# The adaLN gate of a hybrid attention layer: from matmul rows on TensorE to column sums on VectorE and GpSimd

## The chip, the core and the metric

The kernel runs on one NeuronCore of a Trainium2 chip. The metric is the time of one execution on the device in microseconds (us). The profile is one further execution, recorded instruction by instruction. In it PE is TensorE (matmuls), DVE is VectorE, ACT is ScalarE, POOL is GpSimd and SP is SyncE, which here only issues transfers (DMA). Each engine works through its own instructions strictly in order; an instruction that waits holds up all that stand behind it on that engine.

## What is computed

One layer of a diffusion backbone: 128 context tokens and 1024 latent tokens, width 1024, each with its own conditioning vector. The part that matters here is the modulation: a vector is passed through SiLU, multiplied by a 1024 x 3072 matrix, and split into shift, scale and gate. Shift and scale act on the input; the gate is used only at the very end.

```python
def modulation(cond, w_mod, b_mod):
    m = (jax.nn.silu(cond) @ w_mod + b_mod)[..., None, :]
    shift, scale, gate = jnp.split(m, 3, axis=-1)
    return shift, scale, gate

    shift, scale, gate = modulation(c, w_mod[l], b_mod[l])
    h = rmsnorm(xs, norm_gain[l]) * (1.0 + scale) + shift
    q_a, k_a, v_a, g_a, q_b, k_b, v_b, g_b = project(h, w_in[l], ...)
    ...
    xs = xs + gate * merge_out(o_a, g_a, o_b, g_b, w_out[l])
```

The same is done for the context tokens with `c_ctx`. So the gate is two vectors (for `c` and `c_ctx`) of 1024 numbers, each a sum over 1024 products. All is fp32.

## The kernel before

Nine token tiles of 128 rows (tile 0 is the context). Projections are made with fp32r operands split in a high and a low part: three matmuls for each of eight slices of the width, 24 matmuls of 128x128 by 128x512 for one *block* (a token tile by 512 columns). The stages are: modulation, norm and the first gates; the queries of mixer A (first sweep, `m = 0`, nine blocks) and of mixer B (second sweep, `m = 1`, nine blocks); keys and values; the second gates; then attention with the output projection. The gate of the adaLN is worked out inside the two query sweeps, where the pool `qt` is open, is written to a row in DRAM (`gate_row`), and is read back (L1057) for the output.

The order of work is written by hand. `block` (L267 ff.) calls `tick` twice, before its first and before its second half, so **a tick is half a block**; the first sweep has ticks 1 to 18 and the second 19 to 36. `later(n, f)` puts `f` into the list of the tick that is n ahead; a tick runs its list in the order in which entries were made. `in_order` at the end fixes each engine's order as the program wrote it.

A query, after its block, goes through `query` (L586 ff.):

- in the next tick (odd) ACT squares the block's result (`sqq`, L594), DVE sums the squares (`ssq`, L596) and scales them (`ms`, L171), and POOL takes the power -1/2 (`rs`, L173);
- two ticks on (odd) DVE multiplies the result by it (`qn`, L601, from PSUM), and by the rope tables (`ra`, L531, and `rb`, L537, both from SBUF);
- the tick after (even) DVE adds the two (`qf`, L612, from SBUF);
- three ticks after that (odd) PE transposes it, four 128x128 transposes into one bank (`ptq`, L622), ACT copies the bank out as the high part (`qo0`, L625) and DVE one tick later takes the low part (`qo1`, L630, from PSUM); both go to DRAM by transfers that ACT issues (L635). The transposes use two banks D and E in alternation (`bank_tr`), so a transpose waits until DVE has read the bank two before it.

In an odd tick DVE's order is therefore `qn`, `ra`, `rb` of one query, then `ssq`, `ms` of the next; in an even tick `qf` and `qo1`. In the last block of a sweep the weights of the next one are split as well (`Weights.split`, L229): ACT casts the high part, DVE subtracts for the low one (L235), eight times; PE needs each in the block that follows.

The gate before the change: SP loads the gate's weights as four tiles of 1 MB (`load_wg`, two early in the first sweep, two in the second) and the biases. Ahead of the fourth and the eighth block of the second sweep, `gate_rows` makes eight matmuls with the SiLU vectors as weights padded to 32 columns, four side by side, into a bank; a tick later ACT copies it out; three ticks later `gate_sum` adds the four groups with one more matmul (`pgs`, into a bank of D and E), DVE adds the bias (`bg`), and SP writes half the row.

## Time and profile before

| | us |
|---|---|
| Runs: median (lowest to highest of 3) | 723.14 (722.96 to 723.36) |
| Profiled execution, first to last instruction | 721.3 |
| The rest of the median, outside of that span | 1.8 |
| PE busy | 698.3 |
| DVE / ACT / POOL busy | 457.6 / 411.7 / 335.3 |
| Gate matmuls on PE: `pgate` 32 passes, `pgs` 4 passes | 2 stretches of 1.92, 2 of 1.02 |

The page reads the profiled execution: busy time, its share of the span, and the number of instructions for each engine. A row of the timeline is the start, the duration, the engine, the source line, the operation, output and input tiles, shapes and, in brackets, how long the engine had been idle before it and what it had waited for. "x4" merges four instructions that follow each other. A row of a group gives the count, the summed busy time and the mean in ns, and then the idle time ahead of it. The granted TensorE clock was 0.993 of full speed on average.

### The profile page before, as it was taken

The page shows a single profiled execution, that of the slowest core. Times are in us where ns is not written, and L with a number is a line of the kernel's source. Part 1 is how long each engine was busy: PE and PEld are TensorE (multiplying, and loading weights), DVE is VectorE, ACT ScalarE, POOL GpSimd, SP SyncE. Part 2 cuts the span into 40 slices and gives each one's busy share as a digit, 9 for nine tenths or more (in the row PEclk, how much of TensorE's full clock was granted, in tenths as well). Part 3 has the DMA queues.
Part 4 walks back from the last instruction along what each step waited for, and adds up shares of the span by engine and source line. Part 5 has one row for each costly group of instructions (what it writes and reads, how often), then busy time and mean ns, then how long its engine had stood idle before and what let it go on. Part 6 is the DMA issues. An engine that isn't in the chain of part 4 may idle for free. (4 is left out here: it accounts for less than half of the span.)

```text
span 721.3 us, 10622 instructions
## 1 busy us (share of the span) xinstructions
PE 698.3 (97%) x3524; PEld 559.7 (78%) x3524; DVE 457.6 (63%) x1007; ACT 411.7 (57%) x829; POOL 335.3 (46%) x355
## 2 busy tenths in 40 slices
PE   5999999999999999999999999999999999999997
PEld 2678988877777788977788888888888888887865
DVE  3466147875675872745866677577666775775653
ACT  5355411411232451158778877877787778877770
POOL 3456013332322340236666555655575557555751
PEclk9999999999999999999999999999999999999999
DMA  8961373348435115440321222121212221212323
GB/s 344 346 219 59 121 278 86 79 94 276 121 85 142 45 60 171 139 143 23 103 67 45 73 67 88 44 81 52 87 54 59 66 87 45 81 53 87 103 65 119
DMA packets 53159, 78.56 MB, mean 109 GB/s; under 512 B 6569, under 2 KB 25449, under 8 KB 52081
## 3 DMA queue, kind: packets, MB, share of 16 engines
q1 hardware_dynamic: 44928, 65.96, 28.1%
q10 hardware_dynamic: 8176, 11.94, 6.3%
q8 instruction: 28, 0.46, 0.3%
q14 instruction: 27, 0.21, 0.1%
HBM read 58.69 MB, written 19.18 MB: 108 GB/s over the span
## 5 line engine op out<-in xcount | busy, mean ns | idle before, releaser
L1108 POOL TENSOR_TENSOR pl<-pe,ph 128x512 fp32r<-128x512 f32 x130 | 167.6, 1292 | 144.7 <-DVE nm L919 67.5
L859 DVE TENSOR_REDUCE mx<-pmx 128x1 f32<-128x384 f32 x192 | 101.4, 552 | 59.5 <-PE pmx L858 58.1
L1100 ACT ACTIVATE pe<-st 128x512 f32<-128x512 f32 x146 | 86.8, 594 | 28.0 <-PE st L1098 27.1
L1104 ACT CAST ph<-pe 128x512 fp32r<-128x512 f32 x146 | 90.6, 621 | 4.8
L1118 PE MATMUL pv<-ph,v_hi 128*128 128x512 f32 x208 | 83.2, 400 | 2.2 <-DVE spare L1142 2.2
L1121 PE MATMUL pv<-pl,v_hi 128*128 128x512 f32 x208 | 82.6, 397 | 0.0
L173 POOL TENSOR_TENSOR rs_q<-ms_q,mhalf 128x8 f32<-128x8 f32 x18 | 34.8, 1931 | 82.1 <-DVE ms_q L171 82.1
L1189 PE MATMUL po<-wo,ogh 128*128 128x512 f32 x216 | 72.5, 394 | 0.2 <-DVE yt L1196 0.2
L919 DVE CUSTOM_DVE_ANT_0 sn<-sn,mask,nsink 128x512 f32<-128x512 f32 (+1 forms) x64 | 46.3, 724 | 38.3 <-PE sn L916 36.5
L858 PE MATMUL pmx<-kha,qt 128*128 128x384 f32 x192 | 61.0, 363 | 0.4 <-ACT pen L905 0.2
L1097 PE MATMUL st<-qt,kha 128*128 128x512 f32 x144 | 58.3, 405 | 1.5 <-ACT pe L1100 0.8
L1098 PE MATMUL st<-qb,kla 68*128 68x512 f32 x144 | 57.6, 400 | 1.1 <-DVE qb L878 1.1
L1120 PE MATMUL pv<-ph,v_lo 128*64 128x512 f32 x146 | 57.9, 396 | 0.0
L1121 PEld LDWEIGHTS pv<-pl,v_hi 128*128 128x128 f32 x208 | 39.4, 189 | 16.7 <-issue 0.2
L905 ACT ACTIVATE pen<-sn,nm 128x512 f32<-128x512 f32 (+2 forms) x72 | 45.0, 626 | 6.5 <-DVE nm L919 3.1
L1093 ACT CAST ph<-st 128x512 fp32r<-128x512 f32 x62 | 36.4, 587 | 19.9 <-PE st L1092 18.7
L1118 PEld LDWEIGHTS pv<-ph,v_hi 128*128 128x128 f32 x208 | 39.4, 189 | 10.5 <-ACT ogh L1154 2.4
L1189 PEld LDWEIGHTS po<-wo,ogh 128*128 128x128 f32 x216 | 40.0, 188 | 6.8 <-DVE yt L1196 0.6
L1094 DVE TENSOR_TENSOR pl<-st,ph 128x512 fp32r<-128x512 f32 x62 | 42.5, 686 | 2.3 <-ACT ph L1093 1.5
L1189 PE MATMUL po<-wo,ogl 128*128 128x512 f32 x108 | 42.6, 394 | 0.0
L594 ACT ACTIVATE sqq<-pq 128x512 f32<-128x512 f32 x18 | 10.8, 599 | 53.3 <-DMA qd<-qo0q 14.4
L858 PEld LDWEIGHTS pmx<-kha,qt 128*128 128x128 f32 x192 | 35.5, 190 | 6.2 <-DVE mx L859 1.4
(216 smaller groups left out, 1700.2 us busy)
## 6 DMA issues: line engine op xcount, KB each, us to landing
qt<-qd SPq DMA_DIRECT2D x36, 256.0 KB, 3.1
wm<-in_w_mod_ss_dram SPq DMA_DIRECT2D x8, 1024.0 KB, 5.1
qd<-qo0q ACTq DMA_DIRECT2D x36, 128.0 KB, 2.4
qd<-qo1q ACTq DMA_DIRECT2D x36, 128.0 KB, 2.4
sgl<-gd SPq DMA_DIRECT2D x36, 128.0 KB, 2.1
out_dram<-yt SPq DMA_DIRECT2D x17, 256.0 KB, 2.1
xn<-in_x_sample_dram SPq DMA_DIRECT2D x8, 512.0 KB, 7.0
wg<-in_w_mod_g_dram SPq DMA_DIRECT2D x4, 1024.0 KB, 7.9
```

Source lines behind the costliest of these rows:

```text
L858: nc.tensor.matmul(pm[:, 0:384], lhs, kha[:, g, 3 * b : 3 * b + 3, :], start=True, stop=True)
L859: nc.vector.tensor_reduce(mx[:, h, b : b + 1], pm[:, 0:384], axis=AX.X, op=ALU.max)
L919: nc.vector.tensor_tensor_reduce(s, s, mask[:, m0 : m0 + n], -1.0, nsink[:, 4 * g + h : 4 * g + h + 1], op0=ALU.add, op1=ALU.min, accum_ou ...
L1097: nc.tensor.matmul(s, kh, qtile[i], start=True, stop=False)
L1098: nc.tensor.matmul(s, kl, qbtile[i], start=False, stop=True)
L1100: nc.scalar.activation(pe, s, AF.Exp)
L1104: nc.scalar.copy(ph, pe)
L1108: nc.gpsimd.tensor_tensor(pl, pe, ph, op=ALU.subtract)
L1118: nc.tensor.matmul(pv, two, ph, start=(b == 0), stop=False)
L1120: nc.tensor.matmul(pv[0:64, :], vl, ph, start=False, stop=False)
L1121: nc.tensor.matmul(pv, two, pl, start=False, stop=last)
L1189: nc.tensor.matmul(po[n], a, wo_parts[KT * n + k][lo], start=(k == KS[0] and p == 0), stop=(k == KS[-1] and p == 2))
```

## The change

The gate leaves TensorE, apart from one transpose. The host hands the gate's part of the weights over transposed, with the two conditioning vectors appended as rows. Tile `wg{j}` then has 128 gate columns as partitions and the 1024 inputs along the row, and a gate column is a sum along the row. `silb` holds both conditioning vectors on all partitions (two loads of 512 KB, SiLU on ACT in ticks 3 and 4). For j = 0 to 7, in tick 6 + 3j (6, 9, 12, ... 27), `gate_columns(j)`:

- asks for the tile of the next column (`load_wg(j + 1)`, for j of 1 to 6; two buffers);
- on DVE multiplies and sums for `c` in one instruction (its result and a read of the accumulator are two rows);
- on POOL multiplies for `c_ctx` into `prod`, which ACT copies two ticks later, summing on the way.

In tick 30 DVE adds the biases; in tick 31 PE transposes the 16 columns (`ptg`, a bank of D and E), ACT copies them out and SP writes `gate_row`.

```diff
-GATE_AT = (3, 7)
+GATE_AT = (6, 3)
...
-        sil32 = qt.tile([P, KT, 32], F32, name="sil32g", bufs=1)
...
-        def gate_sum(n, grow):
-            pgs = bank_tr(f"pgs{n}")
-            nc.tensor.matmul(pgs[0:2], sel, grow, start=True, stop=True)
-            nc.vector.tensor_tensor(bg[n], pgs[0:2], bg[n], op=ALU.add)
-            nc.sync.dma_start(gate_row[:, 512 * n : 512 * n + 512], bg[n])
-        def gate_rows(n):
-            pg = bank_mm(f"pgate{n}")
-            for k in range(KT):
...
+        silb = qt.tile([P, 2, D], F32, name="silb", bufs=1)
+        gcol = qt.tile([P, 2, KT], F32, name="gcol", bufs=1)
+        gbias = qt.tile([P, KT], F32, name="gbias", bufs=1)
+        for c in range(2):
+            nc.sync.dma_start(silb[:, c], w_mod_g[D + c : D + c + 1, :].to_broadcast([P, D]))
+        nc.sync.dma_start(gbias, cols[:, 40:48])
+        wg = {}
+
+        def load_wg(j):
+            wg[j] = qt.tile([P, D], F32, tag="wg", name=f"wg{j}")
+            nc.sync.dma_start(wg[j], w_mod_g[P * j : P * j + P, :])
+
+        def gate_silu(c):
+            nc.scalar.activation(silb[:, c], silb[:, c], AF.Silu)
+
+        def gate_columns(j):
+            if 0 < j < KT - 1:
+                load_wg(j + 1)
+            junk = qt.tile([P, D], BF16, tag="junk", name=f"junk{j}", bufs=1)
+            nc.vector.tensor_tensor_reduce(junk, wg[j], silb[:, 0], 1.0, 0.0, op0=ALU.mult, op1=ALU.add,
+                                           accum_out=gcol[:, 0, j : j + 1])
+            prod = qt.tile([P, D], F32, tag="prod", name=f"prod{j}", bufs=1)
+            nc.gpsimd.tensor_tensor(prod, wg[j], silb[:, 1], op=ALU.mult)
+            later(2, lambda: nc.scalar.activation(prod, prod, AF.Copy, accum_out=gcol[:, 1, j : j + 1]))
+
+        def gate_turned():
+            pt = bank_tr("ptg")
+            nc.tensor.transpose(pt[0:16, 0:P], gcol.rearrange("p c j -> p (c j)"), ident_r.bitcast(F32))
+            grow = qt.tile([16, P], F32, name="grow", bufs=1)
+            nc.scalar.copy(grow, pt[0:16, 0:P])
+            nc.sync.dma_start(gate_row.rearrange("c (j n) -> (c j) n", n=P), grow)
+
+        for j in range(2):
+            load_wg(j)
+            later(3 + j, lambda j=j: gate_silu(j))
+        for j in range(KT):
+            later(GATE_AT[0] + GATE_AT[1] * j, lambda j=j: gate_columns(j))
+        end = GATE_AT[0] + GATE_AT[1] * (KT - 1) + 3
+        later(end, lambda: nc.vector.tensor_tensor(gcol, gcol, gbias.unsqueeze(1).to_broadcast([P, 2, KT]), op=ALU.add))
+        later(end + 1, gate_turned)
...
-                if m == 1 and t in (ts[GATE_AT[0]], ts[GATE_AT[1]]):
-                    gate_rows(len(wg) // 2 - 1)
...
-    return {"cols": cols, "w_mod_ss": ss, "w_mod_g": w_mod[0][:, 2 * D :]}
+    return {"cols": cols, "w_mod_ss": ss, "w_mod_g": np.concatenate([w_mod[0][:, 2 * D :].T, c.reshape(1, D), c_ctx.reshape(1, D)])}
```

Since the entries for the columns are made before any query's, a column stands first in its tick on DVE and POOL. Three places show what that does to the order. In the names, the number behind `q0_` or `q1_` is the token tile, and the last number is a running one that differs between the programs.

DVE, in the last block of the first sweep (ticks 17 and 18), before:

```order
L596 TENSOR_REDUCE ssq0_8_1514<-sqq0_8_1512 128x8
L171 TENSOR_SCALAR ms_q0_8_1516<-ssq0_8_1514 128x8
L235 TENSOR_TENSOR wloqb_0_1530<-rawqb_0_1416,whiqb_0_1529 128x512
L235 TENSOR_TENSOR wloqb_1_1537<-rawqb_1_1418,whiqb_1_1536 128x512
L612 TENSOR_TENSOR qfq0_7_1540<-ra_q0_7_1505,rb_q0_7_1507 128x2x4x64
L630 TENSOR_TENSOR qo1q0_5_1499<-ptq0_5_1493,qo0q0_5_1498 128x512
L235 TENSOR_TENSOR wloqb_2_1547<-rawqb_2_1420,whiqb_2_1546 128x512
L235 TENSOR_TENSOR wloqb_3_1554<-rawqb_3_1422,whiqb_3_1553 128x512
```

and with the change:

```order
L608 TENSOR_REDUCE ssq0_8_1539<-sqq0_8_1537 128x8
L171 TENSOR_SCALAR ms_q0_8_1541<-ssq0_8_1539 128x8
L235 TENSOR_TENSOR wloqb_0_1555<-rawqb_0_1434,whiqb_0_1554 128x512
L235 TENSOR_TENSOR wloqb_1_1562<-rawqb_1_1436,whiqb_1_1561 128x512
L576 ISA junk4_1567,gcol_1092<-wg4_1454,silb_1091 128x1024
L576 ISA gcol_1092 128x1
L624 TENSOR_TENSOR qfq0_7_1571<-ra_q0_7_1529,rb_q0_7_1531 128x2x4x64
L642 TENSOR_TENSOR qo1q0_5_1523<-ptq0_5_1517,qo0q0_5_1522 128x512
L235 TENSOR_TENSOR wloqb_2_1578<-rawqb_2_1438,whiqb_2_1577 128x512
L235 TENSOR_TENSOR wloqb_3_1585<-rawqb_3_1440,whiqb_3_1584 128x512
```

The fifth column (`junk4`, and the read of its sum) has come between the second and the third of the weights' low parts.

POOL, over the same stretch of the first sweep and into the second, before (powers alone):

```order
L173 TENSOR_TENSOR rs_q0_5_1325<-ms_q0_5_1323,mhalf_106 128x8
L173 TENSOR_TENSOR rs_q0_6_1380<-ms_q0_6_1378,mhalf_106 128x8
L173 TENSOR_TENSOR rs_q0_7_1461<-ms_q0_7_1459,mhalf_106 128x8
L173 TENSOR_TENSOR rs_q0_8_1518<-ms_q0_8_1516,mhalf_106 128x8
L173 TENSOR_TENSOR rs_q0_0_1605<-ms_q0_0_1603,mhalf_106 128x8
```

and with the change:

```order
L173 TENSOR_TENSOR rs_q0_5_1342<-ms_q0_5_1340,mhalf_106 128x8
L579 TENSOR_TENSOR prod2_1360<-wg2_1257,silb_1091 128x1024
L173 TENSOR_TENSOR rs_q0_6_1403<-ms_q0_6_1401,mhalf_106 128x8
L579 TENSOR_TENSOR prod3_1458<-wg3_1356,silb_1091 128x1024
L173 TENSOR_TENSOR rs_q0_7_1485<-ms_q0_7_1483,mhalf_106 128x8
L173 TENSOR_TENSOR rs_q0_8_1543<-ms_q0_8_1541,mhalf_106 128x8
L579 TENSOR_TENSOR prod4_1569<-wg4_1454,silb_1091 128x1024
L173 TENSOR_TENSOR rs_q0_0_1636<-ms_q0_0_1634,mhalf_106 128x8
```

Two of three powers are followed by a product of 1024 elements a partition.

DVE in ticks 29 and 30 with the change, ahead of PE's transpose of the columns in tick 31 (before, `gcol` is not there and the rest stands in the same order):

```order
L608 TENSOR_REDUCE ssq1_5_1922<-sqq1_5_1920 128x8
L171 TENSOR_SCALAR ms_q1_5_1924<-ssq1_5_1922 128x8
L595 TENSOR_TENSOR gcol_1092<-gcol_1092,gbias_1093 128x16
L624 TENSOR_TENSOR qfq1_4_1941<-ra_q1_4_1912,rb_q1_4_1914 128x2x4x64
L642 TENSOR_TENSOR qo1q1_2_1906<-ptq1_2_1900,qo0q1_2_1905 128x512
```

The bias add now stands ahead of the `qf` and `qo1` of tick 30, and PE's `ptg` of tick 31 needs it; `ptg` takes one of the two banks, so the transposes `ptq1_3` behind it take the bank that this `qo1q1_2` reads.

On SP the change puts `silb` (two loads), the biases and two tiles of `wg` ahead of the first sweep's rope tables; the loads of `wg2` and `wg3`, which wait for their buffers, ahead of the second sweep's weights; and the write of `gate_row` in tick 31 ahead of the 16 loads of the key and value weights.

More of the change, by code (lines that the diff above doesn't have):

```diff
@@ L553, in hybrid_step @@
             w.pools = [(qt, KT)] * KT
-        sil32 = qt.tile([P, KT, 32], F32, name="sil32g", bufs=1)
-        nc.gpsimd.memset(sil32, 0.0)
-        nc.vector.tensor_copy(sil32[:, :, 0:2], silc.rearrange("p (c k) -> p k c", c=2))
-        sel = qt.tile([P, 2], F32, name="selg", bufs=1)
-        group_sum(sel, ident_r.bitcast(F32))
-        wg, bg = [], []
-        def gate_sum(n, grow):
-            pgs = bank_tr(f"pgs{n}")
-            nc.tensor.matmul(pgs[0:2], sel, grow, start=True, stop=True)
-            nc.vector.tensor_tensor(bg[n], pgs[0:2], bg[n], op=ALU.add)
-            nc.sync.dma_start(gate_row[:, 512 * n : 512 * n + 512], bg[n])
@@ L569, in gate_rows @@
-        def gate_rows(n):
-            pg = bank_mm(f"pgate{n}")
-            for k in range(KT):
-                a = 32 * (k % 4)
-                nc.tensor.matmul(pg[a : a + 32], sil32[:, k, :], wg[2 * n + k // 4][:, k % 4, :],
-                                 start=(k < 4), stop=(k >= 4), tile_position=(0, a))
-            grow = qt.tile([P, 512], F32, tag="grow", name=f"grow{n}", bufs=1)
-            later(1, lambda: nc.scalar.copy(grow, pg))
-            later(3, lambda: gate_sum(n, grow))
@@ L579, in load_wg @@
-        def load_wg(i):
-            n, b = divmod(i, 2)
-            wg.append(qt.tile([P, 4, 512], F32, tag="wg", name=f"wg{i}"))
-            nc.sync.dma_start(wg[i], w_mod_g[512 * b : 512 * b + 512, 512 * n : 512 * n + 512].rearrange(
-                "(k p) n -> p k n", p=P))
+        silb = qt.tile([P, 2, D], F32, name="silb", bufs=1)
[3 more added lines that the diff above has]
+            nc.sync.dma_start(silb[:, c], w_mod_g[D + c : D + c + 1, :].to_broadcast([P, D]))
@@ L646, in hybrid_step @@
                 pq = bank_mm(f"pq{m}_{t}")
-                if m == 1 and t in (ts[GATE_AT[0]], ts[GATE_AT[1]]):
-                    gate_rows(len(wg) // 2 - 1)
-                if (m, t) in ((0, ts[-2]), (1, ts[GATE_AT[0]])):
-                    n = len(wg) // 2
-                    load_wg(2 * n)
-                    load_wg(2 * n + 1)
-                    if n == 0:
-                        bgt = qt.tile([34, 512], F32, name="bg", bufs=1)
-                    bg.append(bgt[32 * n : 32 * n + 2])
-                    nc.sync.dma_start(bg[n], b_mod[:, 2 * D + 512 * n : 2 * D + 512 * n + 512].to_broadcast([2, 512]))
                 if t == ts[-2]:
```

## The prediction

> **What bounds the kernel now.** I read the page first, then the timeline of TensorE (PE) over the query stage (about 89 to 202 us), then VectorE (DVE), GpSimd (POOL) and ScalarE (ACT) over the same stretch.

> ```profile
> PE 698.3 (97%) x3524; PEld 559.7 (78%) x3524; DVE 457.6 (63%) x1007; ACT 411.7 (57%) x829; POOL 335.3 (46%) x355
> ```

> PE sets the end. A projection block is 24 matmuls; the turn of an earlier query (four transposes, `ptq`, L622) opens it, so the starts of the turns are PE's clock:

> ```profile
> 111.09 0.60 PE L622 MATMUL ptq<-ident_r,qfq 128*128 128x128 f32 x4
> 117.03 0.60 PE L622 MATMUL ptq<-ident_r,qfq 128*128 128x128 f32 x4
> ...
> 153.03 0.60 PE L622 MATMUL ptq<-ident_r,qfq 128*128 128x128 f32 x4
> 159.05 1.92 PE L573 MATMUL pgate<-wg,sil32g 128*32 128x512 f32 x16
> 160.90 0.66 PE L622 MATMUL ptq<-ident_r,qfq 128*128 128x128 f32 x4
> 166.88 0.60 PE L622 MATMUL ptq<-ident_r,qfq 128*128 128x128 f32 x4
> 167.64 1.02 PE L565 MATMUL pgs<-grow,selg 128*2 128x512 f32 x2 [0.15 <-DVE qo1q L630]
> ...
> 174.19 0.60 PE L622 MATMUL ptq<-ident_r,qfq 128*128 128x128 f32 x4
> 180.12 0.60 PE L622 MATMUL ptq<-ident_r,qfq 128*128 128x128 f32 x4
> 187.99 0.66 PE L622 MATMUL ptq<-ident_r,qfq 128*128 128x128 f32 x4
> 193.98 0.60 PE L622 MATMUL ptq<-ident_r,qfq 128*128 128x128 f32 x4
> 201.76 0.63 PE L622 MATMUL ptq<-ident_r,qfq 128*128 128x128 f32 x4 [0.47 <-DVE qo1q L630]
> ```

> A plain block lasts 117.03 - 111.09 = 5.94 us. I call the turns 1 to 18 in this order: turn 1 at 111.09, turn 6 opens the second sweep, turn 7 is six blocks after turn 1.

> DVE does five rows of 0.6 to 0.7 us a query, and one wait:

> ```profile
> 113.88 0.69 DVE L601 TENSOR_TENSOR qnq<-pq,rs_q 128x512 f32<-128x512 f32 x1 [1.53 <-POOL rs_q L173]
> 114.60 0.69 DVE L531 TENSOR_TENSOR ra_q<-qnq,tcos 128x512 f32<-128x512 f32 x1
> ...
> 115.88 0.68 DVE L596 TENSOR_REDUCE ssq<-sqq 128x8 f32<-128x512 f32 x1
> 116.60 0.17 DVE L171 TENSOR_SCALAR ms_q<-ssq 128x8 f32<-128x8 f32 x1
> 116.68 0.69 DVE L612 TENSOR_TENSOR qfq<-ra_q,rb_q 128x512 f32<-128x512 f32 x1
> 117.28 0.68 DVE L630 TENSOR_TENSOR qo1q<-ptq,qo0q 128x512 fp32r<-128x512 f32 x1
> 118.89 0.69 DVE L601 TENSOR_TENSOR qnq<-pq,rs_q 128x512 f32<-128x512 f32 x1 [0.93 <-POOL rs_q L173]
> ...
> 122.39 1.94 POOL L173 TENSOR_TENSOR rs_q<-ms_q,mhalf 128x8 f32<-128x8 f32 x1 [3.54 <-DVE ms_q L171]
> ```

> Its loop is 118.89 - 113.88 = 5.01 us: from `ms` to `qn` 2.29 (POOL's power takes 1.94 of it), then `qn`, `ra`, `rb`, `ssq`, 2.72. So DVE has 0.93 us a block in hand, and no more.

> **What goes.** Four blocks held gate matmuls. Their length over 5.94: 153.03 to 160.90 gives 1.93; 166.88 to 174.19, 1.37; 180.12 to 187.99, 1.93; 193.98 to 201.76, 1.84 (0.47 of it a wait for a bank whose turn `pgs` had shifted). Together **-7.07 us** of PE's own time. Nothing else of it was on PE's path.

> **What comes, priced.**

> ```profile
> L919 DVE CUSTOM_DVE_ANT_0 sn<-sn,mask,nsink 128x512 f32<-128x512 f32 x48 | 36.4, 757 | 27.0 <-PE sn L916 26.8 <-ACT pen L905 0.2
> L919 DVE CUSTOM_DVE_ANT_0 sn<-sn,mask,nsink 128x384 f32<-128x384 f32 x16 | 10.0, 624 | 11.3 <-PE sn L916 9.7 <-ACT ph L1104 1.4
> ...
> L1144 POOL TENSOR_TENSOR spare<-spare,sgl x36: 730/738/746, 341.2 to 703.2; 128x256 f32<-128x256 f32 x36
> ...
> L382 ACT ACTIVATE sq<-xn x9: 1044/1056/1057, 8.0 to 43.6; 128x1024 bf16<-128x1024 f32 x9
> L382 ACT ACTIVATION_READ_ACCUMULATOR sq<-xn x9: 186/187/198, 9.0 to 44.6; 128x1 f32 x9
> ```

> The multiply-and-sum of a column block on DVE is the same instruction as L919 on 1024 elements: 757 + 4 x (757 - 624) = 1.29 us. A plain two-input operation gives a floor: twice L531's 0.69, 1.38, less one fixed part. I take **1.25** from start to next start. The ceiling is twice the streamed part, 2.3, if this operand mix runs at half the rate; no row here has it. ACT's summing copy is 1.06 + 0.19 = 1.25 us and each SiLU about the 1.06; ACT is 57% busy and its copies fall into its waits for PE, or delay the squares by 1.25, which DVE, later still, doesn't feel. POOL's product has 1024 elements: 512 take 1.29 (rows below), 256 take 0.74, so 1.29 + 2 x 0.55 = **2.4 us**, at most 2 x 1.29 = 2.58.

> POOL itself has room: 1.94 + 2.4 fit in a block. But what it does to DVE is in these rows of the attention stage:

> ```profile
> 356.67 1.66 DVE L1015 TENSOR_TENSOR wo_big<-wraw,wo_big 128x512 fp32r<-128x512 f32 x1
> 358.26 0.75 DVE L919 CUSTOM_DVE_ANT_0 sn<-sn,mask,nsink 128x512 f32<-128x512 f32 x1
> 358.93 1.15 DVE L1014 CAST wo_big<-wraw 128x512 fp32r<-128x512 f32 x1
> ...
> 356.45 1.33 POOL L1108 TENSOR_TENSOR pl<-pe,ph 128x512 fp32r<-128x512 f32 x1 [1.34 <-ACT ph L1104]
> 358.50 1.29 POOL L1108 TENSOR_TENSOR pl<-pe,ph 128x512 fp32r<-128x512 f32 x1 [0.72 <-ACT ph L1104]
> ```

> A DVE subtraction of two SBUF tiles, 0.69 elsewhere, takes 1.66 when POOL began first, and a 0.42 us cast takes 1.15: both end a little after POOL's operation does. L919, with one input in PSUM, keeps its 0.75. So while a product runs, DVE's operations on two SBUF tiles stand still: `ra`, `rb`, `qf`, the tables, the weights' low parts, and the new columns. `qn` and `qo1` read PSUM and go on.

> **DVE's loop with a column.** The power ends 2.26 after `ms`. A tick is half a block; columns come every third tick. Even tick: column, `qf`, `qo1` fill the wait; the product runs from 2.26 to 4.66, so `ra` starts at 4.7 in place of 3.0: **6.7 us**. Odd tick: `qf`, `qo1`, column end at 2.55; the product then runs to 4.95: **7.0 us**. Three blocks carry two columns: 6.7 + 7.0 + 5.0 = 18.7 against PE's 17.8. DVE falls behind by 0.9 in three blocks, and by more at the places that follow.

> *First sweep.* The two rope tables now stand behind 2 MB of gate input on SP.

> ```profile
> 99.99 0.68 DVE L546 TENSOR_TENSOR tcos<-tcos,gain 128x512 f32<-128x512 f32 x1
> ...
> 106.56 0.17 DVE L171 TENSOR_SCALAR ms_q<-ssq 128x8 f32<-128x8 f32 x1
> ...
> wg<-in_w_mod_g_dram SPq DMA_DIRECT2D x4, 1024.0 KB, 7.9
> ```

> 1 MB lands in 7.9 us among others; part passes while DVE waits anyway. Bounds 0 and 6 us; I take 2.3. The second `ms` is then at 108.9, and the next ones at 115.6, 122.6, 127.6, 134.3, 141.3 (loops even, odd, plain, even, odd). Turn 3 needs the `qo1` that ends 1.3 behind the ms of 122.6: 123.9, against 122.97 on PE (two blocks after 111.09); turn 4 needs column, `qf`, `qo1` behind 127.6: 130.15, against 129.8; turn 6 needs `qf`, the second tables (1.2 us) and `qo1` behind 141.3: 143.8, against 140.8 today (five blocks after 111.09). Late by **3.0**.

> *The weights' low parts.* This is the largest term.

> ```profile
> 139.96 1.29 DVE L235 TENSOR_TENSOR wloqb<-rawqb,whiqb 128x512 fp32r<-128x512 f32 x2
> ...
> 142.38 3.69 DVE L235 TENSOR_TENSOR wloqb<-rawqb,whiqb 128x512 fp32r<-128x512 f32 x6
> ...
> 143.11 0.50 PE L249 MATMUL pq<-wloqb,h 128*128 128x512 f32 x1
> ...
> 137.27 1.21 ACTq L635 DMA_DIRECT2D qd<-qo1q  x2
> ...
> 139.02 4.25 ACT L233 CAST whiqb<-rawqb 128x512 fp32r<-128x512 f32 x8
> ```

> Already PE waits for the third low part (143.11: 0.3 late). Column 4 now stands between the second and third. `qn` starts at 143.8, so the eighth `ms` is at 146.5: two low parts to 147.8, the column to 149.05; POOL, whose power ended at 148.8, takes the inputs until 151.45; `qf` and `qo1` to 152.65; the third low part at 153.3. PE, which now takes it at 143.11, is 10.2 late: **7.2 more**. (Without any blocking this place costs 2.5: 1.25 for the column, 1.25 for ACT's copy between `qo0` and the issues of 137.27.)

> *The turn of the columns.* `gate_turned` sits ahead of turn 12 and takes a bank in the alternation, so turn 12 needs the `qo1` of the tick just before. The six low parts end at 156.4; counted on, the ms are at 159.1, 163.1 (the context query has no rotation), 169.4 (its power waits for a product, then ACT's squares), 176.1, 183.1, 188.1. Bias add, `qf` and `qo1` end at 189.5; PE, 10.2 late at turn 7, is there at 157.3 + 5 x 5.94 = 187.0: **2.5**, the transpose within it.

> *After it* the second boundary looks like the first does now: **0.4** (147.09 - 140.76 - 5.94).

> *SP.* The KV weights wait behind the gate's row:

> ```profile
> 171.47 9.84 SPq L221 DMA_DIRECT2D rawkv<-in_w_in_dram  x16
> ```

> Begun 0.5 us after turn 12, all 16 are out 10.3 after it, and land some us later; ACT's first cast comes two blocks and 4.2 us after it (139.02 is 4.2 behind its turn), 16.1. Hidden, with about 4 us to spare.

> **Sum.** -7.07 + 3.0 + 7.2 + 2.5 + 0.4 = **+6.0**. The profiled span is 721.3, the median of the runs 723.14, 1.8 more. 721.3 + 6.0 + 1.8 = **729.1 us**. Bounds: start 0 gives about 727, start 6 gives 733; a product of 2.58 adds 0.2 a column, 1.5; the order in which DVE and POOL get the inputs moves 0.6 at the boundary. Own range 725 to 735.

> **Rivals.**

> *The column runs at half rate* (14%). For it: no row has two fp32 SBUF tiles with a running sum; L919 has PSUM and bf16. Against: L531 streams two SBUF tiles at full rate. At 2.3 us the loops are 8.6 and 8.0, turn 6 comes at 149.5, the third low part at 160.1 (17.0 late), turn 12 waits 6.2: -7.1 + 17.0 + 6.2 + 0.4 = +16.5, **739.6 us**. [...]

> *The product doesn't hold DVE* (13%), the other side: if the product costs DVE's loop less than (17.8 - 15.0) / 2 = 1.4 us a column, DVE keeps PE's pace. Left are 0.3 at the start, 2.5 at the boundary, 1.75 at turn 12, 0.4: -7.07 + 4.95 = -2.1, **721.0 us**. For it: POOL's power never slowed `qf` (0.69 throughout). Against: power reads 8 elements, the product 1024, like L1108.

> *The loads come late* (5%): SP's later loads wait for columns to be read, and KV's stand behind the gate row. From 4 us of lateness on each us is PE's: 8 late gives **733**.

> **Chances.** Forecast 68% (725 to 735). Faster by over 0.2% (what a measurement can tell here, 1.4 us): most of the second rival and the low tail, 14%. Within 0.2%: 6%. Slower: 80%. Range 722 to 738, leaving out about 20%.

> **What would show it.** `ra` rows of 2 us and more behind a product; the third `wloqb` about 10 us later than now; turns 3, 4, 6 and 12 waiting for DVE, 7 the most; PE idle for some 13 us more, half of it before that `wloqb`. It is wrong if `ra` stays 0.69 and starts 0.7 after `qn`, or if the columns last 2.3.

## The result, and the profile after

The changed kernel takes **736.69 us** (median of four runs, 735.19 to 737.48), the kernel before 723.14 (722.96 to 723.36). The ratio is 1.0179, with a 95% interval of 1.0158 to 1.0199: slower, by 13.5 us. The profiled execution of the changed kernel took 735.19 us, with a span of 733.4, which is 12.1 more than the 721.3 of the profile before; it was the fastest of the four.

The page of the changed kernel, first the busy time of each engine:

```profile
PE 695.2 (95%) x3489; PEld 559.3 (76%) x3489; DVE 475.5 (65%) x1018; ACT 421.2 (57%) x846; POOL 356.7 (49%) x362
```

PE is busy for 3.1 us less and the span is 12.1 us longer, so PE is idle for some 15 us more. The timeline of PE over the query stage shows where (columns: start, length, operation; in brackets the idle time ahead of it and what ended it). The turns are counted as in the prediction.

```profile
111.88 0.63 PE L634 MATMUL ptq<-ident_r,qfq 128*128 128x128 f32 x4 [1.64 <-issue]
...
124.87 0.66 PE L634 MATMUL ptq<-ident_r,qfq 128*128 128x128 f32 x4 [0.95 <-DVE qo1q L642]
131.68 0.66 PE L634 MATMUL ptq<-ident_r,qfq 128*128 128x128 f32 x4 [0.67 <-DVE qo1q L642]
...
145.40 0.65 PE L634 MATMUL ptq<-ident_r,qfq 128*128 128x128 f32 x4 [1.67 <-DVE qo1q L642]
147.69 0.51 PE L248 MATMUL pq<-whiqb,h 128*128 128x512 f32 x1 [1.63 <-ACT whiqb L233]
148.79 0.50 PE L249 MATMUL pq<-wloqb,h 128*128 128x512 f32 x1 [0.60 <-DVE wloqb L235]
...
154.52 0.79 PE L249 MATMUL pq<-wloqb,h 128*128 128x512 f32 x1 [3.39 <-DVE wloqb L235]
155.11 0.63 PE L250 MATMUL pq<-whiqb,h 128*128 128x512 f32 x1
155.53 0.63 PE L248 MATMUL pq<-whiqb,h 128*128 128x512 f32 x1
...
160.96 0.60 PE L634 MATMUL ptq<-ident_r,qfq 128*128 128x128 f32 x4
...
212.15 0.50 PE L249 MATMUL pk<-wlokv,h 128*128 128x512 f32 x1 [1.35 <-DVE wlokv L235]
...
214.56 0.50 PE L249 MATMUL pk<-wlokv,h 128*128 128x512 f32 x1 [0.75 <-DVE wlokv L235]
```

Turns 3, 4 and 6 wait, as the prediction said, and so does turn 12 (0.84 us, behind 0.29 for the columns' sum); the longest wait is the one for the third low part. But three things stand there that the prediction did not have: PE waits at turn 1, the matmuls from 155.1 to 159.4 are spaced 0.43 us apart in place of 0.23, and PE waits twice at the second weights' boundary.

Turn by turn, the lateness of the changed kernel against the kernel before gives this sum:

| piece | forecast | measured |
|---|---|---|
| stage one, up to the end of the block ahead of turn 1 | 0 | 111.88 - 1.64 - 111.09 = -0.85 |
| first sweep, to turn 6 | +3.0 | 145.40 - 140.76 + 0.85 = +5.5 |
| third low part of W_QB | +7.2 | (154.52 - 143.11) - (145.40 - 140.76) = +6.8 |
| the block behind it, to turn 7 | 0 | (160.96 - 147.09) - (154.52 - 143.11) = +2.5 |
| the four gate blocks gone | -7.07 | -7.2 |
| turn 12 | +2.5 | +1.5 |
| second boundary, to turn 16 | +0.4 | +2.7 |
| key stage and rest | 0 | +1.2 |
| sum | +6.0 | +12.1 |

The -0.85 of stage one cannot be put down to the change. The kernel before, in its profile, had a granted clock of 0.79 from 16 to 24 us, the changed one 1.00; and without the wait at turn 1, that point lies between 110.0 and 111.7 in the profiles of all the kernels below.

On DVE the rows are the ones expected. A column takes 1.21 to 1.22 us, `ra` behind a product 2.2, and the `qf` behind product 4 stands until that product ends:

```profile
132.66 2.19 DVE L531 TENSOR_TENSOR ra_q<-qnq,tcos 128x512 f32<-128x512 f32 x1
...
149.27 1.21 DVE L576 CUSTOM_DVE_ANT_0 junk<-wg,silb 128x1024 bf16<-128x1024 f32 x1
150.41 0.07 DVE L576 DVE_READ_ACCUMULATOR2_ANT gcol<- 128x1 f32 x1
150.41 2.85 DVE L624 TENSOR_TENSOR qfq<-ra_q,rb_q 128x512 f32<-128x512 f32 x1
```

and POOL, over the same time:

```profile
129.43 2.48 POOL L173 TENSOR_TENSOR rs_q<-ms_q,mhalf 128x8 f32<-128x8 f32 x1 [3.72 <-DVE ms_q L171]
131.88 2.42 POOL L579 TENSOR_TENSOR prod<-wg,silb 128x1024 f32<-128x1024 f32 x1
...
150.20 2.51 POOL L579 TENSOR_TENSOR prod<-wg,silb 128x1024 f32<-128x1024 f32 x1
```

The product begun at 150.20 ends at 152.71 and `qf` at 153.26: DVE's sum of two SBUF tiles waits for POOL's.

The slow matmuls are a matter of PE's clock. Windows of 2 us (busy time of each engine, then the granted clock of PE, the DMA share and GB/s):

```profile
146.00:148.00 2.00, 0.37 (x2) 0.19 (x1) 1.97 (x5) 1.47 (x3) 0.00 (x0) 1.00 0.57 131
148.00:150.00 2.00, 1.40 (x5) 1.02 (x5) 2.00 (x4) 2.00 (x5) 1.71 (x1) 0.88 0.00 0
150.00:152.00 2.00, 1.13 (x3) 0.33 (x1) 2.00 (x3) 1.75 (x4) 2.00 (x2) 0.50 0.00 0
...
156.00:158.00 2.00, 2.00 (x6) 1.61 (x5) 2.00 (x4) 0.68 (x2) 0.00 (x0) 0.50 0.32 102
...
160.00:162.00 2.00, 2.00 (x12) 1.65 (x11) 1.97 (x5) 0.40 (x1) 1.58 (x1) 1.00 0.00 0
```

PE was idle for 3.9 of the 5.1 us from 143.7 to 148.8; from about 149.4 its clock is at one half, and it comes back about 5 us after the matmuls run without a gap again. The same happens in the key stage: PE waits 2.50 us up to 241.77, the granted clock is 0.50 from 242 to 245, and the matmuls there are 0.43 apart. The fall came 5.7 us after the first wait began, with matmuls between waits of at most 1.67 us, and in the key stage behind one wait of 2.50; the return took 5.0 and 3.3 us.

The other three runs of the changed kernel had mean clocks of 0.983 to 0.989 against the profiled 0.991, and spans of 734.5 to 735.7. The median is 1.5 us over the profiled execution, for which the prediction had added nothing. The kernel before, beside the experiments, had mean clocks of 0.991 to 1.000 in all its executions.

### The profile page after: what moved, and what is told of

It reads as the page before. It is cut to its first block, busy times and chain, and to the rows that moved or that the text cites. A ratio compares the mean times of both kernels' runs of the same rounds, so it can differ in the third digit from the quotient of the medians.

```text
span 733.4 us, 10612 instructions
## 1 busy us (share of the span) xinstructions
PE 695.2 (95%) x3489; PEld 559.3 (76%) x3489; DVE 475.5 (65%) x1018; ACT 421.2 (57%) x846; POOL 356.7 (49%) x362
## 5 line engine op out<-in xcount | busy, mean ns | idle before, releaser
L173 POOL TENSOR_TENSOR rs_q<-ms_q,mhalf 128x8 f32<-128x8 f32 x18 | 36.5, 2027 | 94.3 <-DVE ms_q L171 91.3
L1123 PEld LDWEIGHTS pv<-pl,v_hi 128*128 128x128 f32 x208 | 39.2, 188 | 16.5
L1095 ACT CAST ph<-st 128x512 fp32r<-128x512 f32 x62 | 36.4, 588 | 19.9 <-PE st L1094 18.6
L407 POOL TENSOR_TENSOR h<-hf,h 128x256 fp32r<-128x256 f32 (+2 forms) x32 | 28.3, 902 | 22.5 <-DVE h L406 22.5
## 6 DMA issues: line engine op xcount, KB each, us to landing
wm<-in_w_mod_ss_dram SPq DMA_DIRECT2D x8, 1024.0 KB, 7.0
```

Source lines behind the costliest of these rows:

```text
L1123: nc.tensor.matmul(pv, two, pl, start=False, stop=last)
```

## The experiments

All were timed beside the kernel before on the same chip. The first four take the change apart, each with something left out; their times are read together at the end of the four.

**no_gate.** The kernel before without its gate matmuls:

```diff
-            pg = bank_mm(f"pgate{n}")
-            for k in range(KT):
...
-            later(1, lambda: nc.scalar.copy(grow, pg))
-            later(3, lambda: gate_sum(n, grow))
+            later(3, lambda: gate_sum(n))
...
-            pgs = bank_tr(f"pgs{n}")
-            nc.tensor.matmul(pgs[0:2], sel, grow, start=True, stop=True)
-            nc.vector.tensor_tensor(bg[n], pgs[0:2], bg[n], op=ALU.add)
```

> The kernel before, with the gate's matmuls, their copies and bias sums left out (the 32 column-block products, the two sums over the groups; the gate's row is the bias alone; loads and writes stay). It measures the term of the removal by itself. The four lengthened blocks of the profile say -7.07 us: 723.14 - 7.1 = 716.0 us. Rival: DVE's loop in the second sweep, which had the cover of the longer blocks, becomes the limit once they are short; then PE waits at the second weights' boundary and less than 7 us is gained, 717 to 719 us.

Measured: 719.35 us, ratio 0.9948 (0.9928 to 0.9968): 3.5 us less, half of the forecast. In the profile turn 16 comes at 200.05 against 207.72, of which 0.86 was there at turn 1 (110.23 against 111.09): 6.8 us of gain, close to the -7.07. It goes behind that. PE's first turn of the key stage

```profile
223.43 0.66 PE L717 MATMUL ptk<-ident_r,k2k 128*128 128x128 f32 x4 [2.67 <-ACT k2k L711]
```

waits 2.67 us, where the kernel before waited 1.17. The last turn of the key stage (267.53 against 273.68) has 5.3 of the 6.8 left, the span 4.3 - 0.9 = 3.4. The rival did not hold at its place (the second boundary costs only 0.4), but a wait did take its part. One thing more differs: the key and value weights are loaded from 139.8, not from 171.5.

**no_both, no_prod, no_col.** The changed kernel without columns and products, without products, and without columns. In no_prod:

```diff
-            nc.gpsimd.tensor_tensor(prod, wg[j], silb[:, 1], op=ALU.mult)
-            later(2, lambda: nc.scalar.activation(prod, prod, AF.Copy, accum_out=gcol[:, 1, j : j + 1]))
+            later(2, lambda: nc.scalar.activation(prod, wg[j], AF.Copy, accum_out=gcol[:, 1, j : j + 1]))
```

and in no_col:

```diff
+        nc.vector.memset(gcol[:, 0], 0.0)
...
-            junk = qt.tile([P, D], BF16, tag="junk", name=f"junk{j}", bufs=1)
-            nc.vector.tensor_tensor_reduce(junk, wg[j], silb[:, 0], 1.0, 0.0, op0=ALU.mult, op1=ALU.add,
-                                           accum_out=gcol[:, 0, j : j + 1])
```

no_both has both edits. In no_prod and no_both ScalarE sums the weights in place of the products.

> The changed kernel without the columns on DVE and without the products on POOL: both halves of the gate are left out; the loads, the SiLUs, ScalarE's sums, the turn of the columns and the row's write stay. Theory: what is left over no_gate is the start (1.6), the small turn (1), the second boundary (2) and ScalarE's sums at the first (1): 723 to 726 us, so that the sums on DVE and POOL are 11 to 14 us of the change's cost. Rival (most of the cost is loads, ScalarE and the turn): 729 us or more.

> The changed kernel without the eight products on POOL: the c_ctx half of the gate is left out (ScalarE sums the weights instead of the products, at the same cost); the columns on DVE stay. Theory (the product holds DVE's SBUF operations): ra stays at 0.69 us, DVE keeps PE's pace, the first sweep is late by about 0.8 (tables only), the third low part by 2.5 to 3 more, PE is never idle long enough to lose its clock, turn 12 waits 1.5: about 722 to 726 us, against 736.7. Rival (the column's own 1.2 us on DVE and the copies on ScalarE carry the cost, the product little): 733 us or more, with the third low part still over 8 us late.

> The changed kernel without the eight columns on DVE: the c half of the gate is left out (zero before the bias); POOL's products and ScalarE's sums stay. Theory (the product is what costs): only 0.2 to 0.5 us a loop and 1.2 us at the weights' boundary come back, ra behind a product still lasts about 2 us; 732 to 735 us. Rival (the column's own time is the cost): 725 us or less.

| kernel | columns | products | median us | ratio to before (95%) |
|---|---|---|---|---|
| no_both | no | no | 723.53 | 1.0008 (0.9988 to 1.0027) |
| no_prod | yes | no | 726.91 | 1.0053 (1.0038 to 1.0069) |
| no_col | no | yes | 734.91 | 1.0179 (1.0149 to 1.0209) |
| changed | yes | yes | 736.69 | 1.0179 (1.0158 to 1.0199) |

no_both and no_col came within what was expected of them, no_prod 0.9 us above its range and far below its rival. Over no_both the columns alone cost 3.4 us, the products alone 11.4, both together 13.2 by the medians; by the ratios, each taken on its own chip, 3.3, 12.4 and 12.4. Beside products, columns cost nothing that the intervals tell apart. So it is POOL's product that costs most, and it costs by holding DVE. DVE's groups from 100 to 225 us (columns: operation and count, then busy us and mean ns of one), without products:

```profile
L531 DVE TENSOR_TENSOR ra_q<-qnq,tcos 128x512 f32<-128x512 f32 x16 | 11.1, 692 | 0.5
```

and with products and no columns:

```profile
L531 DVE TENSOR_TENSOR ra_q<-qnq,tcos 128x512 f32<-128x512 f32 x16 | 20.1, 1255 | 0.5
```

Sixteen `ra` take 9.0 us more, though DVE makes no columns in that kernel. (Its profiled execution was the slowest of its four, 739.20; turn 4 waits 2.96 us there, for squares that stand behind ScalarE's writes, as in tabs_first below.)

What no_both has over no_gate, 4.2 us, is the cost of the things around the sums. Its waits at the second boundary are those of the changed kernel, without a column in it:

```profile
198.27 0.50 PE L249 MATMUL pk<-wlokv,h 128*128 128x512 f32 x1 [1.32 <-DVE wlokv L235]
200.68 0.49 PE L249 MATMUL pk<-wlokv,h 128*128 128x512 f32 x1 [0.74 <-DVE wlokv L235]
```

**row_act.** The gate row's write moved to another queue, so that the KV weights do not stand behind it:

```diff
-            nc.sync.dma_start(gate_row.rearrange("c (j n) -> (c j) n", n=P), grow)
+            nc.scalar.dma_start(gate_row.rearrange("c (j n) -> (c j) n", n=P), grow)
```

> The changed kernel with one edit: the gate row is written from ScalarE's queue in place of SP's, so that the 16 loads of rawkv on SP no longer stand behind it. In the changed kernel the loads are issued from 192.0 to 201.6, ScalarE's writes of the queries take 2.3 to 2.6 us an issue in that time in place of 1.1, its squares come 2.4 to 3.0 late, and PE waits 1.35 + 0.75 at the KV weights. Theory (that is what the second boundary's 2.7 us come from): the loads are issued from about 166 on, the two waits fall to 0.5 or less together, 2 us less at turn 16; 734 to 735 us against 736.7. Rival (the second boundary is late because DVE is still late from the columns): waits of 2 us stay, no change.

Measured: 739.84 us, ratio 1.0238 (1.0220 to 1.0256), 3 us slower than the changed kernel, where 2 us less were expected. The cause was right and the gain was not. The loads are issued from 165.66 to 176.7, and the waits at the second boundary are gone: turn 16 is 6.34 behind turn 15 in place of 8.63. But ScalarE's writes and squares are now held up where DVE had no time to give, two blocks ahead of turn 12:

```profile
175.00 0.69 DVE L608 TENSOR_REDUCE ssq<-sqq 128x8 f32<-128x512 f32 x1 [4.37 <-ACT sqq L606]
```

and PE waits there for the columns' sum:

```profile
194.81 0.37 PE L584 MATMUL ptg<-ident_r,gcol 128*16 128x128 f32 x1 [3.80 <-DVE gcol L595]
195.93 1.12 PE L634 MATMUL ptq<-ident_r,qfq 128*128 128x128 f32 x4 [0.74 <-DVE qo1q L642]
204.21 0.60 PE L634 MATMUL ptq<-ident_r,qfq 128*128 128x128 f32 x4
```

The block behind that wait lasts 8.28 us in place of 5.94: the halved clock again (0.50 from 196 to 200 us).

**fill.** Matmuls that add zero, in the places where PE idled:

```diff
+            if (m, t, k) == (1, 1, 0):
+                fill(out, 7, True)
...
+            if (m, t, k) == (1, 1, 2):
+                fill(out, 14)
...
+            if (m, t, k) == (0, 0, KT - 1):
+                fill(out, 7)
...
+        for _ in range(11):
+            nc.tensor.matmul(pf, zero, h_tile[0, 0, 0][:, 0, :], start=True, stop=True)
```

> The changed kernel with matmuls added where PE idles: a zero stationary operand times a ready tile, 7 at the end of the first sweep, 7 ahead of the second sweep's first block and 14 ahead of its third low part (all add zero to the sum), and 11 ahead of the key stage's first turn (into a bank that nobody reads). About 39 x 0.23 = 9 us more work for PE. Theory (PE's clock is halved because it idled): the third low part comes no earlier, 154.5 us, but the block behind it runs at 0.23 us a matmul in place of 0.43: turn 7 comes 2.4 us earlier, at 158.5, and the key stage's first block gains 1.2; 731 to 734 us against 736.7. Rival (the slow stretch is from something that runs beside PE, not from its idling): matmul spacing stays 0.43 us behind the waits and the time stays or grows by up to 2 us.

Measured: 735.88 us, ratio 1.0181 (1.0165 to 1.0196). The step that it tests came out as forecast:

```profile
154.60 0.50 PE L577 MATMUL pq<-wloqb,h 128*128 128x512 f32 x1 [0.91 <-DVE wloqb L235]
...
155.17 0.39 PE L574 MATMUL pq<-whiqb,h 128*128 128x512 f32 x1
...
158.62 0.60 PE L653 MATMUL ptq<-ident_r,qfq 128*128 128x128 f32 x4
```

The third low part is no earlier, the spacing is 0.23, and turn 7 comes 2.34 us earlier. So PE's idling is what halves its clock here: with the idle time filled, the granted clock stays at 1.00 from 142 to 162 us. At turn 12 PE waits 1.16 us for the columns' sum, so only 1.4 of the 2.34 are left: DVE sets that point. At the fourth turn of the key stage PE is 1.9 us ahead of the changed kernel (254.29 against 256.20), 1.1 of which it had at turn 17 (223.44 against 224.52); the full clock in the key stage is worth the other 0.8, where 1.2 was expected.

The total shows none of it; it is above the 731 to 734 us expected. This profile has a stretch of half clock at the start of the attention stage (0.51 from 330 to 335 us) that the changed kernel's profile lacks, and the two spans are 733.5 and 733.4. Up to the attention stage the clock was worth 1.9 us of the change's 13.5.

**tabs_first.** The first two rope tables ahead of the gate's input:

```diff
+        tabs = {0: rope_tables(qt, 0, 2)}
         silb = qt.tile([P, 2, D], F32, name="silb", bufs=1)
...
-        tabs = {0: rope_tables(qt, 0, 2)}
```

> The changed kernel with one edit: the first two rope tables are asked for ahead of the gate's 2 MB. Theory (the first sweep is late because the tables are): PE's wait of 1.64 us at the first turn goes, every ms of the first sweep comes 1 to 2 us earlier, and since DVE sets turn 6, the third low part too: 735 us, 1.5 less. Rival (the column ahead of the tables, or the start of stage one, is what is late): turn 1 still waits over 1 us.

Measured: 736.44 us, ratio 1.0198 (1.0175 to 1.0221), no gain. Turn 1 no longer waits (111.31), but turn 4 waits 3.18. In ScalarE's timeline, one pair of issues of query writes takes 9.0 us from the first's start to the second's end (1.1 is usual), while SP issues the weights' loads (120.66 to 125.12); the profile names these loads as what ended the wait behind it:

```profile
118.50 9.00 ACTq L648 DMA_DIRECT2D qd<-qo0q  x2
127.55 1.06 ACT L581 ACTIVATE prod<-prod 128x1024 f32<-128x1024 f32 x1 [9.08 <-DMA rawqb<-in_w_in_dram]
```

The squares stand behind these issues in ScalarE's order and start at 128.92, and DVE waits 3.06 us for them.

**both_dve.** Both sums on DVE, nothing on POOL:

```diff
+            nc.vector.tensor_tensor_reduce(junk, wg[j], silb[:, 1], 1.0, 0.0, op0=ALU.mult, op1=ALU.add,
+                                           accum_out=gcol[:, 1, j : j + 1])
-            prod = qt.tile([P, D], F32, tag="prod", name=f"prod{j}", bufs=1)
-            nc.gpsimd.tensor_tensor(prod, wg[j], silb[:, 1], op=ALU.mult)
-            later(2, lambda: nc.scalar.activation(prod, prod, AF.Copy, accum_out=gcol[:, 1, j : j + 1]))
```

> The changed kernel with both sums of a column on DVE (a second multiply-and-sum of 1.22 us with the c_ctx row) and nothing on POOL and ScalarE for them. The whole gate is computed. Theory (a product on POOL costs DVE as much as doing the sum itself): a loop with a column is 5.0 + 2.4 less the 0.93 that DVE waits anyway, 6.5 us, against some 6.85 measured; about 0.35 x 8 = 2.8 us less: 733 to 735 us. Rival (POOL's product takes a good part of the work off DVE): slower than 737 us.

Measured: 734.46 us, ratio 1.0155 (1.0135 to 1.0174), 2.2 less than the changed kernel by the medians, within the expectation; the two intervals overlap, so that it may be less. Doing POOL's share on DVE is no dearer than letting POOL do it.

**skip_b.** row_act with no column at W_QB's boundary, and with the turn of the columns at tick 39:

```diff
-GATE_AT = (6, 3)
+GATE_TICKS = (6, 9, 12, 15, 21, 24, 27, 30)
...
-        end = GATE_AT[0] + GATE_AT[1] * (KT - 1) + 3
+        end = 38
```

> row_act with the columns at ticks 6, 9, 12, 15, 21, 24, 27, 30 in place of 6 to 27 in steps of 3, so that none stands between the second and third low part of W_QB, and with the sums turned at tick 39. Theory (column 4 and its product at the boundary cost 6.8 us there, and the idling that follows 2.5 of PE's clock): the third low part comes 5 us behind the kernel before instead of 11.4, turn 7 at about 153, and PE keeps its clock there: 727 to 731 us. Rival (DVE, late from the first sweep's columns, is the limit whatever stands at the boundary): the third low part over 9 us late, 734 us or more.

Measured: 738.79 us, ratio 1.0212 (1.0188 to 1.0236). Turn 7 came at 157.08; counted from turn 1, which came later here (113.08), that is 5.1 us less than in the changed kernel. This is less than expected: the third low part (first row below) was still 9.2 behind the kernel before, 2.0 of which were there at turn 1, and PE's clock was halved ahead of it (0.62 from 150 to 152 us). Turn 16 has nothing left of it (219.64 against 218.59). It was lost at the small turn, which now stands behind DVE's low parts of the second boundary:

```profile
152.36 0.79 PE L249 MATMUL pq<-wloqb,h 128*128 128x512 f32 x1
...
216.31 0.27 PE L584 MATMUL ptg<-ident_r,gcol 128*16 128x128 f32 x1 [1.07 <-DVE gcol L595]
219.64 1.11 PE L634 MATMUL ptq<-ident_r,qfq 128*128 128x128 f32 x4 [3.06 <-DVE qo1q L642]
```

The theory failed. Both signs of the rival are there (over 9 us late, over 734 us), though what kept the time up was the small turn at its new place, which neither had. Moving a piece only moved the wait.

**spread, spread_t.** both_dve with one column in two blocks, none at a boundary, the turn last (spread_t: with the tables first, as in tabs_first):

```diff
-GATE_AT = (6, 3)
+GATE_TICKS = (6, 10, 14, 23, 27, 31, 39, 40)
...
+        end = 42
...
-            nc.sync.dma_start(gate_row.rearrange("c (j n) -> (c j) n", n=P), grow)
+            nc.scalar.dma_start(gate_row.rearrange("c (j n) -> (c j) n", n=P), grow)
```

> The whole gate on DVE (two sums a column, as in both_dve) at ticks 6, 10, 14, 23, 27, 31, 39, 40: one column in two blocks, none at a weights' boundary, the last two behind the query's blocks where DVE waits for ScalarE's writes, the turn of the columns at tick 43 behind all turns of queries, and the row written from ScalarE's queue. Theory (DVE's time a block is what the change ran out of): two blocks take DVE 5.0 + 6.5 = 11.5 us against PE's 11.9, so PE waits only at the start (1.6 to 3), 1 to 2 at W_QB and 0 to 2 at W_KV, and nothing ahead of turn 12: 719.4 (no gate at all) + 3 to 6 = 722 to 725 us. Rival (the loads, ScalarE's queue and the small turn cost as much as the sums): 730 us or more.

> spread with the first two rope tables asked for ahead of the gate's input on SP. Theory: the wait at turn 1 goes, 1.5 us less than spread if no other wait takes its place. Rival (tabs_first showed one: the loads behind them hold up ScalarE's writes and squares, 3.18 us at turn 4): the same time as spread or more.

Measured: 729.25 us (1.0082, 1.0065 to 1.0098) and 729.17 us (1.0077, 1.0058 to 1.0097). 7.4 us came back, but not the 12 to 15 of the theory. In spread PE waits for nothing from turn 7 to the second boundary, and 1.9 and 0.35 at the two boundaries, as expected. Two longer waits are left ahead of the key stage. At turn 1 a column stands ahead of the `qf` that PE needs, behind late tables; with the tables first (spread_t) this wait is gone, but turn 5 waits 1.33 instead. At the last turn, which the theory did not have, the last two columns stand ahead of the `qo1` that PE needs:

```profile
112.85 0.63 PE L633 MATMUL ptq<-ident_r,qfq 128*128 128x128 f32 x4 [2.84 <-issue]
...
216.54 1.12 PE L633 MATMUL ptq<-ident_r,qfq 128*128 128x128 f32 x4 [4.69 <-DVE qo1q L641]
```

**spread2, spread2_t.** The same with these two moved:

```diff
-GATE_TICKS = (6, 10, 14, 23, 27, 31, 39, 40)
+GATE_TICKS = (7, 11, 15, 23, 27, 31, 41, 42)
...
-        end = 42
+        end = 44
```

> spread with its two remaining waits moved: the columns at ticks 7, 11, 15, 23, 27, 31, 41, 42 (the first behind the first turn's sum in place of ahead of it; the last two behind the turn that waited 4.69 us for them), the turn of the columns at tick 45. Theory (only DVE's place in the order is left): PE's 2.84 at turn 1 and 4.69 at the last turn fall below 1 together, 729.3 - 5 to 6.5 = 723 to 724.5 us, the time of the kernel before. Rival (the last columns hold up the last writes of the queries, and the key stage behind them): a gain of 3 us or less, 726 us or more.

> spread2 with the rope tables asked for ahead of the gate's input. Theory: the rest of the wait at turn 1 goes, 0 to 1.5 us less than spread2. Rival (as in spread_t, a wait of 1.3 us at turn 5 for ScalarE's squares takes its place): the same as spread2 within 0.7 us.

Measured: spread2 723.33 us, ratio 1.0003 (0.9990 to 1.0017), the time of the kernel before, as its theory said. spread2_t **721.20 us, ratio 0.9973 (0.9961 to 0.9984)**: 0.3% less than the kernel before, a small gain, but the interval lies below 1, and 1.9 us over the kernel that computes no gate at all. Its waits of PE from 89 to 245 us, all of them (columns: who waits for whom, us in total, times, longest):

```profile
PE ptg L584 <- DVE gcol L595: 1.8, 1, 1.8
PE ptk L728 <- DVE klp L746: 1.4, 1, 1.4
PE pq L249 <- DVE wloqb L235: 1.4, 2, 0.8
PE ptk L728 <- ACT k2k L722: 0.8, 1, 0.8
PE pk L249 <- DVE wlokv L235: 0.5, 1, 0.5
```

and, for the changed kernel:

```profile
PE ptq L634 <- DVE qo1q L642: 4.1, 4, 1.7
PE pq L249 <- DVE wloqb L235: 4.0, 2, 3.4
PE ptk L729 <- issue: 2.5, 1, 2.5
PE pk L249 <- DVE wlokv L235: 2.1, 2, 1.4
PE ptq L634 <- issue: 1.6, 1, 1.6
PE pq L248 <- ACT whiqb L233: 1.6, 1, 1.6
PE ptg L584 <- DVE gcol L595: 0.3, 1, 0.3
```

spread2_t has 5.9 us of waits in place of 16.2; the kernel before has 3.3. No turn of a query waits any more. The tables' place, worth nothing in tabs_first and spread_t, is worth 2.1 us here, more than the 1.5 at most that was expected: it pays once no later wait takes it up.

## Why the prediction was right in its direction and wrong in its size

The forecast was 729.1 us and the time is 736.69, 7.6 more. In the pieces of the table, the first sweep has 2.5 of that, the block behind the third low part 2.5, the second boundary 2.3, the key stage 1.2, and the median over the profiled execution 1.5; stage one, the low parts, the gate blocks and turn 12 take 2.4 back. The mechanism on which the forecast was built held; four steps around it failed. The rival of the half rate gave 739.6 us, nearer to the measured time than the forecast, but that is chance: what it assumed did not happen.

*The product holds DVE*: right, and shown. `ra` lasts 2.2 us behind a product, `qf` 2.85; without products `ra` is 0.69 and 9.8 us come back (736.69 to 726.91). The rival that the product does not hold DVE falls.

*The column*: right. 1.21 to 1.22 us and 0.08 for its read, against 1.25 forecast; the rival of the half rate, 2.3 us, falls. That this operand mix runs at half the rate was an assumption of the author's, and no run shows it: the columns' means are 1.217 us here and 1.218 and 1.225 in both_dve.

*The weights' low parts*: right, +6.8 against +7.2.

*The small turn*: +1.5 against +2.5, since PE itself came later.

*What goes*: -7.2 at its place, as forecast. What failed is that all of it reaches the end (key stage and rest at 0), for which the prediction, with "Nothing else of it was on PE's path", gave no reason. In no_gate only 3.5 of it do. 1.5 go to a longer wait in the key stage, whose first turn hangs on ScalarE behind the last query writes; the rest goes in the attention stage, at whose start no_gate's profile has a granted clock of 0.50 from 315 to 320 us, and the kernel before's 0.73 from 320 to 325. That the clock is what takes this rest is argued from these windows. In the changed kernel the wait at the key stage's first turn is 2.50 in place of 1.17, which accounts for the +1.2 of the table.

*The first sweep*: the mechanism was right and the size was not, +5.5 against +3.0. The tables came at 103.06 in place of 99.99 + 2.3. By the forecast's chain the first `qf`, behind a column, ended at 110.9, just ahead of PE's 111.09; stage one ended 0.85 earlier and the chain ran 1.0 later (the second `ms` at 109.87 in place of 108.9), so that turn 1 waited 1.64. Where the forecast took a plain loop of 5.0 there was one of 5.66 (123.45 to 129.11), because squares came 0.56 late while SP issued loads. So DVE was 1.6 late against the forecast at turn 6; the other 0.85 is PE's earlier start, which it spent waiting.

*The second boundary*: the step that failed is "After it the second boundary looks like the first does now: 0.4", and "Hidden, with about 4 us to spare". It cost 2.7, and its 2.3 over the forecast are a term that the sum did not have. The data is there in time, as forecast. But while SP issues its 16 loads, a pair of ScalarE's issues of query writes takes 2.61 us in place of 1.1 to 1.2, and DVE waits 2.97 us for the squares behind them:

```profile
194.76 2.61 ACTq L647 DMA_DIRECT2D qd<-qo1q  x2
197.42 0.60 ACT L606 ACTIVATE sqq<-pq 128x512 f32<-128x512 f32 x1 [4.02 <-DMA qd<-qo0q]
...
198.05 0.69 DVE L608 TENSOR_REDUCE ssq<-sqq 128x8 f32<-128x512 f32 x1 [2.97 <-ACT sqq L606]
```

Here too the length is that of a pair of issues, the second held back. In the kernel before, DVE waits for squares in the same way:

```profile
179.69 0.69 DVE L596 TENSOR_REDUCE ssq<-sqq 128x8 f32<-128x512 f32 x1 [3.37 <-ACT sqq L594]
```

But there the loads go out from 171.5 to 181.3, and the boundary's block begins only at 201.76, so DVE can make it up. With the change they stand behind the gate row and go out from 192.0 to 201.6, and that block begins at 209.96. row_act, which moves the loads, and no_both, which has no columns, show that it is the loads' place and not the columns; how a load holds up an issue no run here shows.

*PE's idling*: not in the sum at all. Every wait was priced at its length. Behind the boundary's waits PE ran at half clock, which cost 2.5 us more, and again in the key stage, where it cost about 0.8; fill shows that idling is the cause. Since DVE sets turn 12, about 1.4 of the 2.5 were still there behind it.

*The sum*: it adds what each place costs, and measured at the same places the pieces do add up. But it does not say what a piece taken away would bring. DVE sets PE's time at turns 1, 3, 4, 6, the low parts and turn 12, so what is gained at one of these places is lost again at the next. Four repairs show it: two of terms in the forecast (tabs_first, skip_b) and two of costs that it left out (row_act, fill). None gained anything that the intervals tell apart from the changed kernel, and row_act lost.

## What to carry to other kernels

Work moved off the engine that sets the end pays only if the engine that takes it has time in every loop, not on average. Here DVE had 0.93 us a block. Both sums on VectorE cost 11 us at one column in one and a half blocks (both_dve), and came out 2 us ahead of the kernel before at one in two blocks, with none at the weights' boundaries or ahead of a turn and the tables first (spread2_t). A product given to GpSimd to spare VectorE spared nothing here, where the two hold each other (`ra` 2.2 us behind a product in place of 0.69, the power 2.5 behind a column in place of 1.94): both sums on VectorE cost no more (734.46 us against 736.69). A wait of the matmul engine is not always priced at its length: behind waits of 3.9 us together, and behind several single ones of 2.4 to 2.9, its next matmuls were slower too (0.43 us apart in place of 0.23), while behind others of 2.5 to 3.2 they were not. And here a repair of one wait brought something only together with those that stand behind it.
